# Turning and summing the second half of the positions inside the loop over tiles, ahead of the up-projections

## The chip, the core and the metric

One core of a Trainium2 chip runs the whole program. The metric is the device time of one execution in microseconds (us). Five engines have queues of their own: TensorE (PE in the profile, with its weight loads as PEld), VectorE (DVE), ScalarE (ACT), GpSimd (POOL) and SyncE (SP). SP and POOL issue DMAs here.

## The reference, cut to what matters

Two decoder layers over 1024 positions of 1024 channels. Each ends with a gated feed-forward block, and the change lies at the head of that block, in both layers:

```python
def conv_ffn(h, w_up, dw_w, dw_b, w_down):
    u = causal_dwconv(h @ w_up, dw_w, dw_b)      # (1024 x 1024) @ (1024 x 5632)
    gate, val = jnp.split(u, 2, axis=-1)
    return (jax.nn.silu(gate) * val) @ w_down
...
        h = rmsnorm(x, ffn_norm_g[layer])
        x = x + conv_ffn(h, ffn_w_up[layer], ffn_dw_w[layer], ffn_dw_b[layer], ffn_w_down[layer])
```

## The kernel before

Every matmul operand is kept as two parts, a high one (rounded, written by an ACT cast) and a low one (the rest, usually a DVE subtraction), and a product is three matmuls: high by high, high by low, low by high (`mm3`, L641). A matmul instruction is 128x128 by 128x512.

**The up-projections** (class `Up`) save multiplications with a two-by-two scheme. The activations, turned so that channels lie on the partitions, are four quarters: B11 and B21 are the two halves of the channels for positions 0 to 511, B12 and B22 the same for positions 512 to 1023. Per block `f` of 128 gate and 128 value columns there are seven products of 12 matmuls (four chunks of 128 channels, three matmuls each). Product 0 uses B11, 1 uses B21, 2 uses B22, 3 uses T1 = B11 - B12, 4 uses T2 = B22 + T1, 5 uses T3 = B12 - B22, and 6 uses -T4 = B21 - T2. `hH` and `hL` hold the high and low parts of B11, B21, T1 (in the place of B12) and B22; `self.T` holds those of T2, T3 and -T4. Blocks 0, 1 and 2 start with `first(f)` (product 0, and product 1 in `second`), which need only positions 0 to 511; `block(f)` does the rest.

**Where the quarters come from.** The step before is an output projection with the residual add, in a loop over eight tiles of 128 positions (`back_all`, L780). After each tile's matmuls, DVE adds them to `x` (L808), ACT squares and sums (L716), DVE and POOL make the factor (L709, L710), and DVE scales the tile (L721). Tiles 0 to 3 are then turned by eight 128x128 PE transposes (L258) into two small PSUM banks (`k.sm()`, named ps0bs in the first feed-forward block and ps2s in the second, two banks in turn); ACT and DVE split them and ACT keeps a plain copy in `rb[t]`. Tiles 4 to 7 are left scaled in `ys[t]`. After the loop `turn_rest` turns them into any of eight PSUM banks (`k.bank()`), and DVE writes the four sums into whole-half buffers `raws`, eight instructions of 128x256 per tile. Then T1 and T2 are split by ACT and DVE, and T3 and -T4 by `split_moved`: ACT writes the high part and its negative, and a DMA issued by POOL adds the source onto it.

**The weights** of block `f` are loaded by SP (`load`, L177); `sums` makes the weight sums of the scheme, with ACT (L193, L194) and four accumulating DMAs on POOL (L199).

A scheduler sets the order on each engine ahead of time from its own estimates; on the chip each engine runs its own list strictly in that order, and an instruction that waits holds up all that stand behind it.

Of the kernel before, what the change touches and what calls it, by code (L numbers as in the profile page):

```python
# [23 lines left out]
P = 128  # L24
# [128 lines left out]
class Up:  # L153
# [69 lines left out]
    def norm(self, t, gain):  # L223
# [7 lines left out]
        if t >= 4:  # L231
            self.ys[t] = y[0]
        else:
            self.rb[t] = m.alloc()
            rb, yv = m.ap(self.rb[t]), m.ap(y[0])
            for g in range(2):
# [3 lines left out]
                h = k.hH[:, g * 4:g * 4 + 4, t * P:(t + 1) * P]  # L240
                l = k.hL[:, g * 4:g * 4 + 4, t * P:(t + 1) * P]
# [3 lines left out]
            m.free(y[0])  # L245
        if t in (1, 3):
            self.load(t // 2)
        if t == 6:
            self.prepare(0)

# [9 lines left out]
    def turn_rest(self):  # L260

        k, m, nc = self.k, self.k.m, self.k.nc
        self.prepare(1)
        self.load(2)
        self.prepare(2)
        raws = [[m.alloc() for _ in range(2)] for _ in range(4)]

        def view(i, t):
            return [m.ap(s).rearrange("p (k s) -> p k s", k=2)[:, :, (t - 4) * P:(t - 3) * P] for s in raws[i]]

        def halves(ap):
            v = ap.rearrange("p (k s) -> p k s", k=4)
            return [v[:, 0:2], v[:, 2:4]]

        for t in range(4, 8):
            yv = m.ap(self.ys[t])
            b12, b22 = k.bank(), k.bank()
            self.turn(b12, yv, 0)
            self.turn(b22, yv, 1)
            rb, w = m.ap(self.rb[t - 4]), m.alloc()  # L280
            r22, t1 = m.ap(w)[:, 0:512], m.ap(w)[:, 512:1024]
            nc.scalar.copy(out=r22, in_=b22)
            h = k.hH[:, 4:8, t * P:(t + 1) * P]
            l = k.hL[:, 4:8, t * P:(t + 1) * P]
            v22 = b22.rearrange("p (k s) -> p k s", k=4)
            nc.scalar.copy(out=r(h), in_=v22)
            V = [view(i, t) for i in range(4)]

            def both(eng, out, a, b, op=ALU.subtract):
                for o, x, y in zip(out, a, b):  # L290
                    eng.tensor_tensor(out=o, in0=x, in1=y, op=op)

            both(nc.vector, V[0], halves(rb[:, 0:512]), halves(b12))
            both(nc.vector, V[2], halves(b12), halves(r22))
            both(nc.vector, V[1], halves(b22), V[0], ALU.add)
            both(nc.vector, V[3], halves(rb[:, 512:1024]), V[1])
            nc.vector.tensor_tensor(out=r(l), in0=v22, in1=h, op=ALU.subtract)
            k.banks += [b12, b22]
            m.free(w)
            m.free(self.ys.pop(t))  # L300
            m.free(self.rb[t - 4])
            if t % 2:
                self.first(t // 2 - 2)
        self.first(2)
        self.split_s12(0)
        for i in (0, 1, 2, 3):
            if i == 0:
                for q, s in enumerate(raws[0]):
                    src = m.ap(s).rearrange("p (k s) -> p k s", k=2)
                    h = k.hH[:, q * 2:q * 2 + 2, 512:1024]  # L310
                    l = k.hL[:, q * 2:q * 2 + 2, 512:1024]
                    nc.scalar.copy(out=r(h), in_=src)
                    nc.vector.tensor_tensor(out=r(l), in0=src, in1=h, op=ALU.subtract)
                    m.free(s)
            elif i == 1:
                self.T[i] = [k.split(s) for s in raws[i]]
            else:
                self.T[i] = [self.split_moved(s) for s in raws[i]]
# [48 lines left out]
    def block(self, f):  # L367
# [27 lines left out]
        if f in self.a1:  # L395
            self.second(f)
# [1226 lines left out]
```

## Time and profile before

| | |
|---|---|
| runs, median of 3 | 2321.15 us (2319.4 to 2325.52) |
| profiled execution: time, span | 2319.02 us, 2317.2 us |
| mean granted TensorE clock | 0.993 |
| PE busy | 2232.6 us of the span |
| DVE busy | 1726.5 us |
| ACT busy | 1262.6 us |
| POOL busy | 561.8 us |

The profiled execution stands 2.13 us below the median of the runs. In the first layer the loop over tiles ends at 356.07 us of the span and in the second at 1661.49 us; what follows each, up to the first products that need the second half, is the place of the change. Times in rows of the profile are microseconds from the span's start; a matmul's own duration (0.39) overlaps the next one's, so PE's pace is read from the distance of the starts.

### The profile page before, as it was taken

The numbers are of one execution on the slowest core, as the hardware profiler recorded it, in microseconds if no ns is written. First come the engines' busy times: TensorE is split into PE (matmuls) and PEld (weight loads), VectorE is DVE, ScalarE is ACT, GpSimd is POOL, SyncE is SP. The second block draws the span as 40 slices with busy tenths as digits, with TensorE's granted clock in tenths as the row PEclk, the third lists the DMA queues.
The fourth block names the chain that finished last, engine by engine and source line by source line (L and its number), as shares of the span: only waits on it lengthen the run. The fifth ranks groups of instructions, "written<-read, shape, count | busy, mean of one in ns | idle before, by whom it ended". The sixth has DMA issues, their size and how long they took to land. (4 is left out here: it accounts for less than half of the span.)

```text
span 2317.2 us, 29706 instructions
## 1 busy us (share of the span) xinstructions
PE 2232.6 (96%) x11076; PEld 1908.4 (82%) x11076; DVE 1726.5 (75%) x2023; ACT 1262.6 (54%) x1978; POOL 561.8 (24%) x551
## 2 busy tenths in 40 slices
PE   8998999999999999999999999989999999999999
PEld 8886887888788888889999999978777888888887
DVE  6879457877686887556888888887668777778863
ACT  6433246555555543436677677765566565655341
POOL 2221012111111000035555555562121121110000
PEclk9999999999999999999999999999999999999999
DMA  5984146767676494321111110034476767666812
GB/s 178 190 174 99 35 127 144 191 144 193 148 186 155 146 386 168 103 80 28 37 28 37 37 37 10 28 106 152 130 162 166 192 149 196 145 177 249 332 51 109
DMA packets 247826, 313.00 MB, mean 135 GB/s; under 512 B 12557, under 2 KB 170753, under 8 KB 247681
## 3 DMA queue, kind: packets, MB, share of 16 engines
q1 hardware_dynamic: 214977, 238.32, 31.0%
q0 software_dynamic: 32704, 72.78, 17.7%
q8 instruction: 87, 1.43, 0.2%
q14 instruction: 58, 0.48, 0.1%
HBM read 181.14 MB, written 60.82 MB: 104 GB/s over the span
## 5 line engine op out<-in xcount | busy, mean ns | idle before, releaser
L199 POOL DMA_DIRECT2D t<-t x176 | 155.8, 978 | 701.2 <-ACT t L194 271.3
L628 ACT CAST t<-t 128x1024 fp32r<-128x1024 f32 x178 | 184.9, 1048 | 223.9 <-DMA hs<-t 62.0
L819 DVE SCALAR_TENSOR_TENSOR t<-t,cst,t 128x1023 f32<-128x1023 f32 (+1 forms) x184 | 236.1, 1286 | 81.9 <-ACT t L817 76.7
L629 DVE TENSOR_TENSOR t<-t,t 128x1024 fp32r<-128x1024 f32 x178 | 219.1, 1237 | 101.0 <-ACT t L628 47.2
L1274 DVE TENSOR_TENSOR_SCAN t<-t 128x127 f32<-128x127 f32 (+7 forms) x128 | 204.1, 1600 | 6.9 <-ACT t L1265 6.8
L644 PE MATMUL ps1s<-wH,hH 128*128 128x384 f32 x448 | 165.8, 370 | 0.0
L646 PE MATMUL ps0b<-hH,t 128*128 128x512 f32 x396 | 154.6, 391 | 3.5 <-DVE t L629 3.4
L644 PE MATMUL ps0b<-hH,t 128*128 128x512 f32 x396 | 155.8, 395 | 1.9 <-DVE t L1104 1.4
L645 PE MATMUL ps0b<-hL,t 128*128 128x512 f32 x396 | 154.7, 391 | 0.0
L710 POOL TENSOR_TENSOR stat<-stat,mhalf 128x8 f32<-128x8 f32 (+1 forms) x65 | 80.2, 1234 | 299.9 <-DVE stat L709 299.7
L646 PE MATMUL ps1s<-wH,hL 128*128 128x384 f32 x448 | 151.1, 337 | 0.0
L1279 POOL TENSOR_TENSOR t<-t,t 128x639 f32<-128x639 f32 (+1 forms) x64 | 108.6, 1697 | 175.1 <-DVE t L1274 103.7
L645 PE MATMUL ps1s<-wL,hH 128*128 128x384 f32 x448 | 150.9, 337 | 0.0
L817 ACT ACTIVATE t<-t,cst 128x1024 f32<-128x1024 f32 x88 | 109.1, 1240 | 66.3 <-DVE t L392 47.4
L645 PE MATMUL ps2b<-t,t 128*128 128x512 f32 x342 | 133.9, 392 | 3.9 <-DMA t<-t 3.9
L644 PE MATMUL ps2b<-t,t 128*128 128x512 f32 x342 | 134.0, 392 | 3.3 <-ACT t L394 1.6
L646 PE MATMUL ps2b<-t,t 128*128 128x512 f32 x342 | 132.7, 390 | 0.0
L1265 ACT ACTIVATE t<-ps1s 128x512 f32<-128x512 f32 (+1 forms) x192 | 95.4, 497 | 54.7 <-PE ps1s L1261 28.3
L1297 ACT CAST t<-ps1s 128x512 fp32r<-128x512 f32 (+1 forms) x160 | 87.3, 546 | 60.9 <-PE ps1s L1293 53.5
L1298 DVE TENSOR_TENSOR t<-ps1s,t 128x512 fp32r<-128x512 f32 (+1 forms) x160 | 100.2, 627 | 21.0 <-ACT t L1297 18.8
L517 ACT CAST hH<-t 128x1024 fp32r<-128x1024 f32 x64 | 64.4, 1051 | 86.4 <-PE ps0bs L645 19.6
L517 ACT CAST hL<-t 128x1024 fp32r<-128x1024 f32 x64 | 64.3, 1051 | 86.3 <-PE ps2s L645 25.3
(348 smaller groups left out, 6480.7 us busy)
## 6 DMA issues: line engine op xcount, KB each, us to landing
t<-in_ffn_w_up_dram SPq DMA_DIRECT2D x88, 512.0 KB
t<-t POOLq DMA_DIRECT2D x176, 256.0 KB, 4.4
t<-hs SPq DMA_DIRECT2D x66, 512.0 KB
hs<-t SPq DMA_DIRECT2D x60, 512.0 KB
t<-in_ffn_w_down_dram SPq DMA_DIRECT2D x66, 256.0 KB
xd<-t SPq DMA_DIRECT2D x24, 512.0 KB
wr<-in_attn_w_qkv_dram SPq DMA_DIRECT2D x24, 512.0 KB
t<-in_ffn_w_up_dram SPq DMA_DIRECT2D x44, 256.0 KB
```

Source lines behind the costliest of these rows:

```text
L199: nc.gpsimd.dma_start(out=out, in_=src, accum_op=ALU.add)
L517: nc.scalar.copy(out=r(m.ap(h)), in_=src)
L628: nc.scalar.copy(out=r(m.ap(h)), in_=m.ap(src))
L629: (eng or nc.vector).tensor_tensor(out=r(m.ap(l)), in0=m.ap(src), in1=m.ap(h), op=ALU.subtract)
L644: mm(out=ps, lhsT=sH, rhs=mH, start=start, stop=False, skip_group_check=onto)
L645: mm(out=ps, lhsT=sH, rhs=mL, start=False, stop=False, skip_group_check=onto)
L646: mm(out=ps, lhsT=sL, rhs=mH, start=False, stop=stop, skip_group_check=onto)
L817: nc.scalar.activation(dst, src, AF.Identity, scale=wcols[2], bias=bias)
L819: nc.vector.scalar_tensor_tensor(out=dst[:, s:], in0=src[:, :S - s], scalar=wcols[2 - s], in1=dst[:, s:], op0=ALU.mult, op1=ALU.add)
L1274: self.nc.vector.tensor_tensor_scan(out=rev, data0=rev, data1=rev, initial=1.0, op0=ALU.mult, op1=ALU.bypass)
L1279: self.nc.gpsimd.tensor_tensor(out=B[:, 0:n - 1], in0=B[:, 0:n - 1], in1=K[:, 1:n], op=ALU.mult)
L1298: nc.vector.tensor_tensor(out=r(aL), in0=ps[:, 0:pos], in1=aH, op=ALU.subtract)
```

## The change

Tiles 4 to 7 are turned inside the loop too (`turn_sums`, called from `norm`), into the two small banks. The sums are made in place of what was there: T1 goes over the copy of B11 in `rb`, -T4 over that of B21, T2 and T3 into a new slot, and T1's and B22's parts go to `hH` and `hL` at once. `turn_rest` now issues `first(0)` ahead of the rest and splits T2, T3 and -T4 tile by tile in pieces of 128x256, high by ACT and low by DVE (`split_t`). `split_moved`, with its four accumulating DMAs of 512 KB a layer, is gone, and so is `raws`. Product 1 of block 2 moves from `turn_rest` into `block(0)`.

```diff
@@ norm
-        if t >= 4:
-            self.ys[t] = y[0]
-        else:
+        if t < 4:
...
+        else:
+            self.turn_sums(t, yv, cs)
+        m.free(y[0])
@@
+    def turn_sums(self, t, yv, cs):
+        k, m, nc = self.k, self.k.m, self.k.nc
+        lo, hi = slice(0, 512), slice(512, 1024)
+        b12, b22 = k.sm(), k.sm()
+        self.turn(b12, yv, 0)
+        self.turn(b22, yv, 1)
+        self.ys[t] = m.alloc()
+        rb, w = m.ap(self.rb[t - 4]), m.ap(self.ys[t])
...
+        h1, l1, h2, l2 = k.hH[:, 0:4, cs], k.hL[:, 0:4, cs], k.hH[:, 4:8, cs], k.hL[:, 4:8, cs]
+        tt = nc.vector.tensor_tensor
+        t1 = rb[:, lo]
+        nc.scalar.copy(out=w[:, hi], in_=b22)
+        tt(out=t1, in0=t1, in1=b12, op=ALU.subtract)
+        nc.scalar.copy(out=r(h2), in_=four(b22))
+        nc.scalar.copy(out=r(h1), in_=four(t1))
+        tt(out=w[:, lo], in0=b22, in1=t1, op=ALU.add)
+        tt(out=w[:, hi], in0=b12, in1=w[:, hi], op=ALU.subtract)
+        tt(out=r(l2), in0=four(b22), in1=h2, op=ALU.subtract)
+        tt(out=r(l1), in0=four(t1), in1=h1, op=ALU.subtract)
+        tt(out=rb[:, hi], in0=rb[:, hi], in1=w[:, lo], op=ALU.subtract)
@@ turn_rest
+        self.first(0)
+        self.prepare(1)
+        self.split_t(1, self.ys, slice(0, 512))
+        self.first(1)
+        self.load(2)
+        self.split_s12(0)
+        self.prepare(2)
+        self.split_t(2, self.ys, slice(512, 1024))
+        self.first(2, False)
+        self.split_t(3, [None] * 4 + self.rb, slice(512, 1024))
@@
+    def split_t(self, i, src, half):
...
+        for t in range(4, 8):
+            for j, (h, l) in enumerate(self.T[i]):
...
+                nc.scalar.copy(out=r(h), in_=x)
+                nc.vector.tensor_tensor(out=r(l), in0=x, in1=h, op=ALU.subtract)
@@ block
-        if f in self.a1:
-            self.second(f)
+        for q in (f, f + 2):
+            if q in self.a1 and q in self.done1:
+                self.second(q)
```

The lists show where this puts the instructions. Lines of the changed program differ: L287 is the transpose (L258 before), L795 the residual add (L808), L708 the scaling (L721), L703 the squares (L716), L615 and L616 the high and low part of a whole split (L628, L629), L270 to L278 are in `turn_sums`, L313 and L314 in `split_t`.

PE in the second layer, before, from tile 7's last matmul on. The rows with t23, t37 and t31 turn tiles 4, 5 and 6, each into banks of its own.

```order
L646 MATMUL ps2b2_13163<-t29_12938,t35_13169 128x512
L258 MATMUL ps2b0_13161<-ident_80,t23_13393 128x128 x8
L258 MATMUL ps2b1_13162<-ident_80,t37_13424 128x128 x8
L258 MATMUL ps2s0_13164<-ident_80,t31_13455 128x128 x4
L258 MATMUL ps2s1_13165<-ident_80,t31_13455 128x128 x4
L644 MATMUL ps2b2_13163<-hH_66,t19_13468 128x512
```

PE in the second layer now, 41 rows behind tile 7's last matmul. t19 is tile 6, t35 tile 7; t43 and t35_13623 are the high and low part of a weight of block 1, t49 that of product 3 of block 0.

```order
L631 MATMUL ps2b1_13174<-hH_66,t43_13622 128x512
L632 MATMUL ps2b1_13174<-hL_67,t43_13622 128x512
L287 MATMUL ps2s0_13176<-ident_80,t19_13503 128x128 x4
L287 MATMUL ps2s1_13177<-ident_80,t19_13503 128x128 x4
L287 MATMUL ps2s0_13176<-ident_80,t35_13563 128x128 x4
L287 MATMUL ps2s1_13177<-ident_80,t35_13563 128x128 x4
L631 MATMUL ps2b2_13175<-hH_66,t49_13680 128x512
L633 MATMUL ps2b1_13174<-hH_66,t35_13623 128x512
```

The turns of tiles 4 to 7 still stand behind tile 7's last matmul in this layer, spread among `first` and `second`, and tile 7's go into the banks that tile 6's have just filled.

DVE in the first layer, before, at the scaling of tile 7 (L721).

```order
L291 TENSOR_TENSOR t30_2473<-t38_2149,t37_2469 128x2x128
L291 TENSOR_TENSOR t26_2474<-t38_2149,t45_2470 128x2x128
L721 SCALAR_TENSOR_TENSOR t31_2433<-t23_137,stat_98,t53_2044 128x1024
L629 TENSOR_TENSOR t51_2464<-t39_2450,t42_2463 128x1024
L629 TENSOR_TENSOR t19_2640<-t25_2166,t48_2639 128x1024
```

DVE in the first layer now, at the same scaling (L708). t32_2453 is the low part of block 0's first weight.

```order
L616 TENSOR_TENSOR t32_2453<-t31_2164,t22_2452 128x1024
L277 TENSOR_TENSOR hL_67<-t33_2207,hH_66 128x4x128
L275 TENSOR_TENSOR t21_2435<-ps0bs0_549,t21_2435 128x512
L274 TENSOR_TENSOR t21_2435<-ps0bs1_550,t33_2207 128x512
L276 TENSOR_TENSOR hL_67<-ps0bs1_550,hH_66 128x4x128
L314 TENSOR_TENSOR t46_2657<-t28_2121,t49_2656 128x2x128
L314 TENSOR_TENSOR t46_2657<-t38_2149,t49_2656 128x2x128
L218 TENSOR_TENSOR t16_2771<-t47_2275,t16_2771 128x512
L696 TENSOR_SCALAR stat_98<-stat_98 128x1
```

Tile 7's factor (L696), which stood 8 rows behind tile 7's residual add, now stands 28 rows behind it, and its scaling (L708) six rows further, behind the sums of tiles 5 and 6 and behind splits of T2, T3, -T4 and weights.

ACT in the first layer, before, around tile 7's squares (L716). t39_2450 is the gate weight of block 2, t25_2166 a weight sum of block 0.

```order
L282 COPY t48_2503<-ps0b1_72 128x512
L286 CAST hH_66<-ps0b1_72 128x4x128
L716 ACTIVATE t31_2433,stat_98<-t23_137 128x1024
L193 ACTIVATE t41_2452<-t39_2450 128x512
L194 ACTIVATE t43_2456<-t39_2450 128x1024
L628 CAST t42_2463<-t39_2450 128x1024
L628 CAST t48_2639<-t25_2166 128x1024
```

ACT in the first layer now, ahead of tile 7's squares (L703). t25_2674<-t16_2445 is the high part of another weight sum of block 0, one that POOL's accumulating DMAs have to finish first.

```order
L615 CAST t25_2674<-t16_2445 128x1024
L273 CAST hH_66<-t33_2207 128x4x128
L313 CAST t49_2656<-t28_2121 128x2x128
L313 CAST t49_2656<-t38_2149 128x2x128
L270 COPY t21_2435<-ps0bs1_550 128x512
L272 CAST hH_66<-ps0bs1_550 128x4x128
L217 CAST t16_2771<-t47_2275 128x512
L703 ACTIVATE t31_2487,stat_98<-t23_137 128x1024
```

ACT in the second layer now, ahead of tile 7's squares. t44_13674 is the gate weight of block 2, whose load takes the slot of a weight of the output projection that tile 7 still uses.

```order
L615 CAST t49_13680<-t22_13278 128x1024
L193 ACTIVATE t25_13676<-t44_13674 128x512
L194 ACTIVATE t28_13684<-t44_13674 128x1024
L615 CAST t40_13691<-t44_13674 128x1024
L703 ACTIVATE t35_13563,stat_98<-t43_13070 128x1024
```

In both layers tile 7's squares now stand behind a row of ACT that needs a transfer, and with them, ahead of them or behind, the copies that the turned tiles need.

More of the change, by code (lines that the diff above doesn't have):

```diff
@@ L260, in turn_rest @@
     def turn_rest(self):
-        k, m, nc = self.k, self.k.m, self.k.nc
[L263 to L273, printed above, removed]
-        for t in range(4, 8):
[L276 to L318, printed above, removed]
```

25 lines of the change are left out of this document (13 added, 12 removed).

## The prediction

> **What bounds the kernel now.** First the page's busy times and its chain of waits: TensorE bounds nearly everything.
>
> ```profile
> span 2317.2 us, 29706 instructions
> PE 2232.6 (96%) x11076; PEld 1908.4 (82%) x11076; DVE 1726.5 (75%) x2023; ACT 1262.6 (54%) x1978; POOL 561.8 (24%) x551
> ```
>
> The change adds no matmul and removes none, so it can only move the time that PE loses. I looked for that with PE's waits, between the end of the loop over tiles and the first products that need positions 512 to 1023, in the first layer and then in the second.
>
> ```profile
> PE ps0bs L645 <- DVE hL L313: 2.9, 1, 2.9
> PE ps0bb L644 <- ACT t L394: 2.4, 1, 2.4
> ...
> PE ps2b L645 <- DMA t<-t: 3.9, 1, 3.9
> PE ps2b L644 <- ACT t L394: 1.6, 1, 1.6
> PE ps2b L644 <- DVE t L808: 1.4, 1, 1.4
> ```
>
> The 3.9 is product 6 waiting for the accumulating DMA of -T4, which the change removes. The timeline of PE gives the full loss, slow clock included.
>
> ```profile
> 356.07 1.04 PE L258 MATMUL ps0b<-ident,t 128*128 128x128 f32 x8
> 379.95 0.80 PE L645 MATMUL ps0bs<-hL,t 128*128 128x512 f32 x1 [2.93 <-DVE hL L313]
> 380.97 0.63 PE L644 MATMUL ps0bs<-hH,t 128*128 128x512 f32 x1
> 381.40 0.63 PE L645 MATMUL ps0bs<-hL,t 128*128 128x512 f32 x1
> 400.95 0.50 PE L644 MATMUL ps0bb<-t,t 128*128 128x512 f32 x1 [2.43 <-ACT t L394]
> 401.29 0.39 PE L645 MATMUL ps0bb<-t,t 128*128 128x512 f32 x1
> 403.58 0.39 PE L646 MATMUL ps0bb<-t,t 128*128 128x512 f32 x1
> 403.81 0.39 PE L644 MATMUL ps0b<-hH,t 128*128 128x512 f32 x1
> ...
> 1661.49 1.91 PE L258 MATMUL ps2b<-ident,t 128*128 128x128 f32 x16
> 1666.23 0.50 PE L644 MATMUL ps2b<-hH,t 128*128 128x512 f32 x1 [1.39 <-DVE t L808]
> 1667.35 0.63 PE L644 MATMUL ps2b<-hH,t 128*128 128x512 f32 x1
> 1710.26 0.50 PE L645 MATMUL ps2b<-t,t 128*128 128x512 f32 x1 [3.87 <-DMA t<-t]
> 1711.95 0.63 PE L644 MATMUL ps2b<-hH,t 128*128 128x512 f32 x1
> 1712.37 0.63 PE L645 MATMUL ps2b<-hL,t 128*128 128x512 f32 x1
> ```
>
> At full clock a matmul takes (403.58 - 401.29)/10 = 0.23 us; longer runs give 0.2267, which I use. From 356.07 to the first matmul behind product 6 of block 0 at 403.81 stand 156 matmuls and 32 turns: 156 x 0.2267 + 4 x 1.04 = 39.6 us in 47.74, so 8.1 us are lost. In the second layer the same from 1661.49 to 1711.95 takes 50.5 us, and 10.9 are lost. **No gain of this change at these places can be above 19.0 us.** The rows 0.63 long, 0.42 apart, are slow clock: such stretches are 8 matmuls long and cost 8 x 0.2 = 1.6 us each.
>
> Then a table by stretches, to see who has time where.
>
> ```profile
> core 0: us, PE busy (x) PEld busy (x) DVE busy (x) ACT busy (x) POOL busy (x), PEclk, DMA share, GB/s
> 319.00:356.00 37.00, 37.00 (x180) 30.76 (x179) 19.82 (x25) 17.93 (x30) 6.30 (x9) 1.00 0.49 141
> 356.00:380.00 24.00, 20.98 (x108) 16.89 (x105) 21.24 (x45) 16.07 (x24) 5.93 (x7) 1.00 0.62 135
> 1632.00:1661.00 29.00, 29.00 (x145) 24.34 (x145) 16.16 (x23) 17.30 (x29) 8.22 (x11) 1.00 0.63 165
> 1661.00:1687.00 26.00, 23.59 (x111) 19.03 (x110) 24.89 (x49) 17.76 (x27) 3.88 (x5) 0.93 0.34 81
> ```
>
> In the loop DVE is half busy; behind it DVE is nearly full (21.24 of 24 us, 24.89 of 26). So DVE is the bound at the head, and what matters is whether the change takes DVE work out of it. The durations of that work:
>
> ```profile
> 355.18 1.22 DVE L629 TENSOR_TENSOR t<-t,t 128x1024 fp32r<-128x1024 f32 x1
> 356.31 1.22 DVE L808 TENSOR_TENSOR t<-ps0b,t 128x1024 f32<-128x1024 f32 x1
> ...
> 375.62 1.41 DVE L291 TENSOR_TENSOR t<-ps0b,t 128x256 f32<-128x256 f32 x4
> 381.62 0.68 DVE L363 TENSOR_TENSOR t<-ps0bs,t 128x512 f32<-128x512 f32 x1
> 382.22 0.68 DVE L218 TENSOR_TENSOR t<-t,t 128x512 fp32r<-128x512 f32 x1
> ```
>
> By distance: 1024 wide 1.13 us, 512 wide 0.60, 256 wide about 0.335.
>
> **The change part by part.** Tile by tile, eight sums of 256 columns (2.7 us) and the whole-half splits give way to six instructions of 512 (3.6 us), which hold two splits; `split_t` adds 24 low parts of 256 on DVE (24 x 0.335 = 8.0 us a layer) for T2, T3 and -T4, of which the removed whole splits did T2 and the accumulating DMAs did T3 and -T4. DVE therefore gets more work a layer, at the place where it is the bound, unless the order puts it under the loop. The lists say where it is.
>
> *First layer.* Of tiles 4 to 7 only tile 4 is turned before tile 7's matmuls end; tile 5's turn stands behind them. Tile 7's residual add can start at about 358.3: tile 7's last matmul now ends near 357.5 (8 turn rows of tile 4 are ahead of it), and a low part of a weight, 1024 wide, is in front. From that add up to tile 7's scaling stand 7 DVE instructions of 1024, 14 of 512, 13 of 256 and one tiny: 7 x 1.13 + 14 x 0.60 + 13 x 0.335 + 0.06 = 20.7 us, to 379.0. Then tile 7 is turned, and four of 512 and two of 256 (3.1 us) follow until the small banks are free again, 382.1. Only there can PE go on with the 24 matmuls whose target is such a bank, and then the 84 up to the end of product 6: 108 x 0.2267 = 24.5 us, 406.6. PE's own cover for this, the 48 matmuls and 16 turn rows since 358.2, is 10.9 + 2.1 us, so it waits. To this I add 1.0 us for a stall between products 5 and 6, where the before has one of 2.43 on the same kind of copy (L394); the bounds are 0.6, one copy,
>
> ```profile
> 387.79 0.57 ACT L388 COPY t<-ps0bs 128x512 f32<-128x512 f32 x1
> ```
>
> and 2.43; I take a value nearer the copy, since ACT has less queued there. That makes 407.6 against 403.81: **+3.8 us** (+3.4 to +5.2).
>
> *Second layer.* All four turns stand behind tile 7's last matmul, so nothing of the sums runs in the loop. DVE starts tile 7's add near 1661.9, and up to tile 7's bank-freeing sum it has 7 x 1.13 + 24 x 0.60 + 10 x 0.335 + 0.06 = 25.8 us: 1687.7. PE's cover is 4.2 us of turns and 39 matmuls, 8.8 us, plus what else does not need a small bank; tile 7's turn must wait for tile 6's sums in the same two banks, which I expect as a wait of 4 to 6 us. Behind it stand 117 matmuls, 26.5 us: 1714.2 against 1711.95, **+2.3 us**. The 3.87 at product 6 is gone in this, and DVE is late in its place.
>
> *Transfers in front of ACT.* In both layers tile 7's squares now stand behind an ACT row that needs a transfer. First layer: the cast of t25_2674 needs POOL's four accumulating DMAs of block 0.
>
> ```profile
> DMA to landing us min/median/max: 3.3/4.4/9.6
> ```
>
> They are issued behind an ACT result at about 364.3; with four in a row they land near 370.7, where ACT comes by at 366.9. Late by 0 to 3.5 us; I take 1.5, as the shortest landing would bring them in time. Second layer: the gate weight of block 2 gets its slot at about 1660.3, when tile 7's weight is done. The nearest load in the trace:
>
> ```profile
> 354.43 0.57 SPq L183 DMA_DIRECT2D t<-in_ffn_w_up_dram  x1
> 359.65 0.63 ACT L193 ACTIVATE t<-t 128x512 f32<-128x512 f32 x1 [0.38 <-DMA t<-in_ffn_w_up_dram]
> ```
>
> 5.2 us, so 1665.5 against 1662.4 in line; 0 to 2.6 late behind DVE's queue, I take 1.0. Together **+2.5** (0 to 6.1).
>
> [...]
>
> *Slow clock.* The rows above show it behind waits of 2.93 and 3.87, and not behind 2.43 (401.29 to 403.58 at full pace). Each layer gets a wait longer than that at the turns: 0 to 2 more stretches each, I take one: 2 x 1.6 = **+3.2** (0 to 6.4).
>
> *Parts at nothing.* The removed `split_moved` frees POOL's queue of four DMAs a layer,
>
> ```profile
> L326 POOL DMA_DIRECT2D t<-t x8: 862/872/1170, 383.5 to 1704.7; - x8
> ```
>
> 8 x 0.87 us of a queue that is 24% busy. ACT's 24 casts of 256 stand for whole-half ones and moved copies, and ACT is at 16 to 18 us of 24 to 26 there. The move of product 1 of block 2 changes only which matmuls are cover, and they are counted. The turns are the same 32.
>
> **Sum**: 3.8 + 2.3 + 2.5 + 3.2 = **+11.8 us**. Against the profiled execution's 2319.02 this is 2330.8; that execution stands 2.13 below the median, so the median becomes 2321.15 + 11.8 = 2333.0. The bounds of the terms give +5.7 to +20.0, 2327 to 2341.
>
> **The rivals.** A measurement of this kernel can tell about 0.3%, 7.0 us: no change is 2314.2 to 2328.1.
>
> *No change that can be told.* Transfers land in time and the clock holds: 3.8 + 2.3 = 6.1, 2327.3. Near as likely is that a DVE instruction or two run earlier than my walk has them. For it: both of these terms start at 0, and the trace has ACT waiting only 0.38 on a weight there. Against it: one late transfer is enough to leave the band.
>
> *Faster.* The sums are found done when PE needs them, since the loop's DVE is half idle (19.82 of 37 us): PE never waits, the whole 19.0 goes, 2302; half of it, 2311.6. It decides when the DVE work from tile 7's add to tile 7's sums in the second layer falls from 25.8 us to the 20.5 that 72 matmuls and the turns cover, that is, when nine or more instructions of 512 ran before that add. Against it: the lists put the turns behind tile 7's last matmul, all four in the second layer, three in the first, and an engine runs strictly in its order.
>
> *The change does not do what it says.* In the second layer "in the loop" is after the loop for all four tiles. This is in my forecast; had it been true of the first layer too, that layer would lose tile 4's 3.6 us more: 2336.6.
>
> *More slow clock.* Two more stretches in each layer, since waits for banks come at tile 6's turn and again at tile 7's: 3.2 more than the forecast, 2336.2. For it: 1667.35 is slow behind waits of only 1.39, where turns had stood ahead. Against it: after 356.07 the turns brought none, as the clock of 1.00 in the row from 356 to 380 shows. [...]
>
> **How the numbers follow.** Forecast 0.49, more slow clock 0.09, not in the loop in the first layer either 0.05: slower 0.63. No change 0.24. Faster 0.13. The range runs from 2314, below which the faster case lies, to 2341, the sum of the upper bounds, above which I leave 0.07; the forecast's own range is 2327 to 2341.
>
> **What would show it.** In the second layer, waits of PE at the turns of tiles 6 and 7 on DVE's sums (L275, L276) of 4 to 6 us together; DVE full from 1662 to about 1690; the matmul behind product 6 near 1714 to 1719 instead of 1711.95, and no DMA wait there. In the first layer the same point at 407 to 412 instead of 403.81, with tile 7's scaling near 379 to 381. ACT waits on a DMA just ahead of tile 7's squares. I am wrong if DVE has done tile 5's and 6's sums before tile 7's add, or if later stalls, of blocks 1 and 2, vanish: each gives back what it was long.

## Result: 1.5% slower, and the profile after

| | before | after |
|---|---|---|
| median | 2322.29 us (4 runs, 2319.4 to 2325.52) | 2357.16 us (4 runs, 2355.3 to 2358.4) |
| ratio, 95% interval | | 1.015 (1.0135 to 1.0165) |
| span of the profiled execution | 2317.2 us | 2353.4 us |
| mean granted clock | 0.993 | 0.985 |

The change costs 34.9 us, where the forecast had 11.8 and an upper end of 20. The page of after shows the same matmuls, with PE busy for 10.2 us longer at a lower granted clock, 12 us more of DVE and no more of ACT; the other 26.0 of the 36.2 us by which the span grew are idle time of PE.

```profile
span 2353.4 us, 29690 instructions
PE 2242.8 (95%) x11076; PEld 1913.2 (81%) x11076; DVE 1738.3 (74%) x2039; ACT 1261.6 (54%) x2010; POOL 557.1 (24%) x543
```

**Where it went.** Four rows of each trace cut the program: the first residual add of the loop over tiles, and ACT's last copy of block 0, in each layer. Before, then after:

```profile
310.39 1.23 DVE L808 TENSOR_TENSOR t<-ps0bb,t 128x1024 f32<-128x1024 f32 x1 [5.27 <-PE ps0bb L646]
404.60 0.57 ACT L399 COPY t<-ps0bb 128x512 f32<-128x512 f32 x1
1624.08 2.58 DVE L808 TENSOR_TENSOR t<-ps2b,t 128x1024 f32<-128x1024 f32 x2 [7.07 <-PE ps2b L646]
1712.18 0.59 ACT L399 COPY t<-ps2b 128x512 f32<-128x512 f32 x1 [3.93 <-PE ps2b L646]
```

```profile
310.80 1.23 DVE L795 TENSOR_TENSOR t<-ps0bb,t 128x1024 f32<-128x1024 f32 x1 [5.49 <-PE ps0bb L633]
417.86 0.59 ACT L386 COPY t<-ps0b 128x512 f32<-128x512 f32 x1
1647.49 2.58 DVE L795 TENSOR_TENSOR t<-ps2b,t 128x1024 f32<-128x1024 f32 x2 [7.07 <-PE ps2b L633]
1742.81 0.59 ACT L386 COPY t<-ps2b 128x512 f32<-128x512 f32 x1 [2.13 <-PE ps2b L633]
```

From cut to cut, the after's time less the before's: 12.8 us at the first layer's head, 10.2 behind it, 7.2 at the second layer's head, 5.6 behind it to the end. **The heads lose 20.0 us and the stretches behind block 0, where nothing was forecast, 15.8.** Of the latter, 9.7 and 5.6 us are lost up to the first sum of the down-projection (L571, now L558: 849.17 and 2155.82 before, 872.11 and 2192.06 after), so they lie in the 21 blocks that follow block 0 in each layer. The same four numbers are given for each experiment below. The first add alone stands between 308.7 and 314.8 us in the profiled executions of these kernels, which are the same up to there; so a difference of 2 us in one of them says little, and in the long stretches behind the heads one of 4 us.

**The heads.** PE's waits of after, in the first layer's head and in the second's:

```profile
PE ps0b L633 <- DVE t L616: 8.4, 2, 8.0
PE ps0bs L287 <- DVE t L708: 3.6, 1, 3.6
PE ps0bs L631 <- DVE t L275: 2.2, 1, 2.2
...
PE ps2s L287 <- DVE t L275: 5.2, 1, 5.2
PE ps2b L631 <- ACT t L615: 4.1, 1, 4.1
PE ps2b L631 <- ACT hH L273: 1.7, 1, 1.7
```

Followed back in the timelines of POOL, ACT, DVE and PE of the first layer:

```profile
362.03 1.76 POOL L199 DMA_DIRECT2D t<-t  x2 [3.51 <-PE ps0b L633]
367.66 2.66 POOL L199 DMA_DIRECT2D t<-t  x3 [3.87 <-DMA t<-t]
371.39 0.86 POOL L199 DMA_DIRECT2D t<-t  x1 [1.07 <-DMA t<-t]
...
374.04 1.04 ACT L615 CAST t<-t 128x1024 fp32r<-128x1024 f32 x1 [6.36 <-DMA t<-t]
378.11 1.06 ACT L703 ACTIVATE t<-t 128x1024 f32<-128x1024 f32 x1 [0.41 <-DVE t L616]
...
375.12 1.23 DVE L616 TENSOR_TENSOR t<-t,t 128x1024 fp32r<-128x1024 f32 x1 [4.83 <-ACT t L615]
385.00 1.28 DVE L708 SCALAR_TENSOR_TENSOR t<-t,stat,t 128x1024 f32<-128x1024 f32 x1 [0.46 <-POOL stat L697]
...
378.13 0.80 PE L633 MATMUL ps0b<-hH,t 128*128 128x512 f32 x1 [7.97 <-DVE t L616]
386.35 1.97 PE L287 MATMUL ps0bs<-ident,t 128*128 128x128 f32 x8 [3.58 <-DVE t L708]
417.66 0.39 PE L631 MATMUL ps0bs<-hH,t 128*128 128x512 f32 x1
```

POOL's sums wait for one another. ACT's cast of a sum waits 6.36 us for the third of those issued from 367.66 on; this is the view of that one alone:

```profile
L199 POOL DMA_DIRECT2D t<-t x1: 1433/1433/1433, 368.9 to 368.9; - x1
  ACT t L615: 6.4, 1
DMA to landing us min/median/max: 5.1/5.1/5.1
```

DVE waits 4.83 for that cast, at the head of its line; PE waits 7.97 for the low part of quite another weight that stands behind on DVE. Tile 7's squares (L703) are behind the same cast on ACT, so its scaling comes at 385.00 and its turn at 386.35. The first matmul behind product 6 is at 417.66.

In the second layer ACT waits 2.71 us for the load of block 2, and PE 4.13 behind it. The 5.22 at tile 7's turn ends with DVE, where no row from 1696.14 to 1707.16 had to wait:

```profile
1688.00 0.63 ACT L193 ACTIVATE t<-t 128x512 f32<-128x512 f32 x1 [2.71 <-DMA t<-in_ffn_w_up_dram]
1690.42 1.05 ACT L703 ACTIVATE t<-t 128x1024 f32<-128x1024 f32 x1
...
1690.57 0.53 PE L631 MATMUL ps2b<-hH,t 128*128 128x512 f32 x1 [4.13 <-ACT t L615]
1707.89 1.11 PE L287 MATMUL ps2s<-ident,t 128*128 128x128 f32 x4 [5.22 <-DVE t L275]
1743.07 0.39 PE L631 MATMUL ps2s<-hH,t 128*128 128x512 f32 x1
```

**Behind block 0.** PE's longest wait there, with the rows of ACT ahead of it:

```profile
440.52 0.63 ACT L193 ACTIVATE t<-t 128x512 f32<-128x512 f32 x1 [6.35 <-DMA t<-in_ffn_w_up_dram]
443.67 1.04 ACT L615 CAST t<-t 128x1024 fp32r<-128x1024 f32 x1 [2.51 <-DMA t<-t]
444.62 0.58 ACT L337 COPY t<-ps0b 128x512 f32<-128x512 f32 x1
...
445.25 0.79 PE L631 MATMUL ps0b<-t,t 128*128 128x512 f32 x1 [2.78 <-ACT t L337]
```

ACT has taken up the weight of a block that is wanted only some 50 us later (by the order of the loads block 5; block 4's last copy is at 489.3), waits for its load, and a copy that PE needs now (L337) stands behind it.

### The profile page after: what moved, and what is told of

The parts are those of the page before. It is cut to its first block, busy times and chain, and to the rows that moved or that the text cites. A ratio compares the mean times of both kernels' runs of the same rounds, so it can differ in the third digit from the quotient of the medians.

```text
span 2353.4 us, 29690 instructions
## 1 busy us (share of the span) xinstructions
PE 2242.8 (95%) x11076; PEld 1913.2 (81%) x11076; DVE 1738.3 (74%) x2039; ACT 1261.6 (54%) x2010; POOL 557.1 (24%) x543
## 4 chain that ended last, share of the span: by engine, by line
PE 50%; DVE 15%; DMA 6%; ACT 4%; issue 3%; POOL 3%; SPq 0%; POOLq 0%; DVEq 0%; ACTq 0%
PE ps2b L631 6%; PE ps2b L633 6%; PE ps2b L632 6%; DVE t L1261 4%; PE ps0b L631 3%; PE ps0b L633 3%; PE ps0b L632 3%; PE ps0bb L631 2%; PE ps2s L631 2%; PE ps2s L633 2%; PE ps2s L632 2%; DVE t L806 2%; PE ps0bb L632 2%; PE ps0bb L633 2%; DMA hs<-t 2%
## 5 line engine op out<-in xcount | busy, mean ns | idle before, releaser
L199 POOL DMA_DIRECT2D t<-t x176 | 155.7, 975 | 749.6 <-DMA t<-in_ffn_w_up_dram 303.1
L615 ACT CAST t<-t 128x1024 fp32r<-128x1024 f32 x174 | 181.0, 1048 | 206.3 <-DMA hs<-t 42.6
L616 DVE TENSOR_TENSOR t<-t,t 128x1024 fp32r<-128x1024 f32 x174 | 214.4, 1237 | 81.5 <-ACT t L615 43.2
L804 ACT ACTIVATE t<-t,cst 128x1024 f32<-128x1024 f32 x88 | 109.0, 1240 | 39.6 <-DVE t L349 27.0
L631 PE MATMUL ps2b<-t,t 128*128 128x512 f32 x306 | 119.8, 392 | 2.9 <-ACT t L380 1.4
L632 PE MATMUL ps2b<-t,t 128*128 128x512 f32 x306 | 119.4, 390 | 0.0
L633 PE MATMUL ps2b<-t,t 128*128 128x512 f32 x306 | 118.7, 390 | 0.0
L631 PE MATMUL ps0b<-t,t 128*128 128x512 f32 x272 | 108.6, 399 | 7.2 <-ACT t L380 4.4
L631 PE MATMUL ps2b<-hH,t 128*128 128x512 f32 x260 | 103.4, 398 | 8.0 <-ACT t L615 4.1
```

Of the source, the lines that this page charges most:

```text
L199: nc.gpsimd.dma_start(out=out, in_=src, accum_op=ALU.add)
L615: nc.scalar.copy(out=r(m.ap(h)), in_=m.ap(src))
L616: (eng or nc.vector).tensor_tensor(out=r(m.ap(l)), in0=m.ap(src), in1=m.ap(h), op=ALU.subtract)
L631: mm(out=ps, lhsT=sH, rhs=mH, start=start, stop=False, skip_group_check=onto)
L632: mm(out=ps, lhsT=sH, rhs=mL, start=False, stop=False, skip_group_check=onto)
L633: mm(out=ps, lhsT=sL, rhs=mH, start=False, stop=stop, skip_group_check=onto)
```

## The experiments

Kernels that start from the changed one are named a, those from the kernel before b. Ratios are to the kernel before, run beside them.

| run | median us | ratio (95%) | head 1 | behind 1 | head 2 | behind 2 |
|---|---|---|---|---|---|---|
| after | 2357.16 | 1.015 (1.0135 to 1.0165) | 12.8 | 10.2 | 7.2 | 5.6 |
| a_act_late | 2346.26 | 1.0106 (1.008 to 1.0132) | 6.4 | 3.2 | 5.2 | 9.6 |
| a_second | 2352.31 | 1.0136 (1.0102 to 1.017) | 10.0 | 8.9 | 4.6 | 7.9 |
| a_pool_low | 2355.36 | 1.0146 (1.0116 to 1.0177) | 9.2 | 9.7 | 8.4 | 7.4 |
| a_late_pool | 2348.96 | 1.0111 (1.0091 to 1.0131) | 6.2 | 6.0 | 5.4 | 11.6 |
| a_after_loop | 2341.53 | 1.0078 (1.0059 to 1.0097) | 4.9 | 10.1 | 0.2 | 7.3 |
| a_early2 | 2338.26 | 1.0064 (1.0049 to 1.008) | 0.3 | 11.2 | -1.2 | 8.9 |
| a_late_prep | 2392.65 | 1.0306 (1.0279 to 1.0332) | 6.3 | 30.6 | 5.2 | 28.1 |
| a_late_prep2 | 2340.26 | 1.0076 (1.006 to 1.0093) | 6.3 | 3.2 | 5.2 | 4.7 |
| a_early2_prep2 | 2330.8 | 1.004 (1.0026 to 1.0054) | 1.3 | 2.2 | 1.3 | 4.7 |
| b_second | 2314.74 | 0.9972 (0.9959 to 0.9986) | -1.9 | 4.2 | -0.2 | -2.7 |
| b_split | 2315.95 | 0.997 (0.9959 to 0.9982) | -0.7 | 2.5 | -2.4 | 0.7 |
| b_both | 2315.37 | 0.9971 (0.9956 to 0.9987) | -1.7 | 0.9 | -4.2 | 1.3 |
| b_pieces | 2317.95 | 0.9986 (0.9975 to 0.9996) | 0.8 | 0.3 | -2.1 | -0.2 |
| b_order | 2393.95 | 1.0313 (1.0294 to 1.0331) | 5.5 | 30.9 | 0.8 | 34.5 |
| b_both_prep2 | 2311.67 | 0.996 (0.9946 to 0.9975) | -0.3 | -1.4 | -2.9 | -3.4 |

### Transfers in front of ACT, and DVE's work

**a_act_late** puts the rows that wait for a transfer behind tile 7's last cast on ACT:

```diff
+        with self.k.tc.issue_after(self.last_cast.ins):
+            self.split_s12(0)
+            self.prepare(2)
```

> The changed kernel, with one thing more: on ACT the split of block 0's first weight sum and the preparation of block 2 (negations and split of its weight) are made to stand behind tile 7's last cast, in both layers. Nothing is computed otherwise. Theory 'transfers in front of ACT': the waits of PE of 7.97 us (first layer) and 4.13 us (second layer), which end with ACT results that stood behind a transfer, fall to under 3 and under 1 us, and the time falls by 8 to 14 us from the changed kernel's 2357, to 2343 to 2349. Rival 'DVE is the bound at the head': PE waits the same time elsewhere, at the turns, and the time stays within 4 us of 2357.

Measured: 10.9 us less than the changed kernel. Squares and rows that wait have changed places; PE's wait of 7.97 is 2.54, that of 4.13 is 0.54. The time left the 4 us that the rival allows, but 11.6 us are still lost at the heads, and PE's longest wait in each is at tile 7's turn:

```profile
377.16 1.12 PE L287 MATMUL ps0bs<-ident,t 128*128 128x128 f32 x4 [3.48 <-DVE t L709]
1689.82 1.12 PE L287 MATMUL ps2s<-ident,t 128*128 128x128 f32 x4 [4.62 <-DVE t L275]
```

**a_pool_low** gives DVE less to do:

```diff
+                eng = nc.vector if i == 1 else nc.gpsimd
+                eng.tensor_tensor(out=r(l), in0=x, in1=h, op=ALU.subtract)
-                nc.vector.tensor_tensor(out=r(l), in0=x, in1=h, op=ALU.subtract)
```

> The changed kernel with the low parts of T3 and -T4 made by POOL instead of DVE: 16 subtractions of 128x256 a layer (5.4 us of DVE a layer) leave DVE. Theory 'DVE is the bound at the head': PE's waits at the turns and on splits fall by 3 to 5 us a layer and the time by 6 to 10 us, to 2347 to 2351. Theory 'transfers in front of ACT': only the part of DVE that stands in front of tile 7's turn counts, 0 to 2 us a layer: 2353 to 2357. If POOL is late with its parts, products 5 and 6 wait for POOL and it is slower than 2357.

Measured: 2355.36 (2351.28 to 2360.37), within the second theory's bounds and outside the first's. No wait of PE in the heads ends with POOL.

**a_late_pool** is both edits at once.

> The first experiment's kernel (no transfer in front of tile 7's ACT rows) with the low parts of T3 and -T4 made by POOL, 5.4 us of DVE less a layer. Theory 'DVE is the bound at the head once the transfers are gone': PE's waits at tile 7's turn (3.5 us in the first layer, 4.6 in the second) and on late splits (2.5 and 3.2) fall by 2 to 4 us a layer, the time by 4 to 8 us to 2338 to 2342. Rival 'the two banks and the order of the turns': within 2 us of 2346. If POOL's rows hold up its transfers or tile 7's factor, up to 6 us slower.

Measured: 2.7 us slower than with a_act_late's edit alone, just outside the 2 us of its rival.

But neither run took time off DVE, and so neither tests what less work there would be worth. The 32 instructions that went to POOL should have freed 32 x 0.335 = 10.7 us. DVE is busy for 1737.8 us in a_pool_low against 1738.3 in the changed kernel, and for 1736.6 us in a_late_pool against 1737.4 in a_act_late. Beside POOL's low parts rows of DVE took longer: the two below took 6.19 us together, where two such rows take 0.75 in the changed kernel (from 380.39 on).

```profile
385.37 6.19 DVE L316 TENSOR_TENSOR t<-t,t 128x256 fp32r<-128x256 f32 x2
385.72 5.20 POOL L316 TENSOR_TENSOR t<-t,t 128x256 fp32r<-128x256 f32 x7
```

What DVE's amount of work is worth is read better from b_split, b_pieces and a_early2 below.

### The parts of the change alone, or undone

**a_second** puts product 1 of block 2 back into `turn_rest`, **b_second** makes that move alone.

```diff
-        self.first(2, False)
+        self.first(2)
...
-        for q in (f, f + 2):
-            if q in self.a1 and q in self.done1:
-                self.second(q)
+        if f in self.a1:
+            self.second(f)
```

> The changed kernel with product 1 of block 2 put back from block(0) into turn_rest, the rest as changed. Theory 'late slot': in the changed kernel the gate weight of block 3 goes into a slot that product 1 of block 2 frees (issued at 400.92 us of the span, against 382.93 before), and the first layer's 10 us that are lost behind block 0 come from that. Then block 3's load is issued near 385 us, the loss behind block 0 falls from 10 to under 4 us a layer and the time falls by 6 to 15 us, to 2342 to 2351. Rival 'chance of the lists': the losses behind block 0 come from where the scheduler happens to put rows that wait for weights, in any version; the time changes by less than 5 us, or by as much with stalls at other blocks. Rival 'cover': the 12 matmuls stand again in the head, where they cover 2.7 us of DVE's work a layer: 5 us less, all of it at the head.

> The kernel before with this one part of the change alone: product 1 of block 2 moves from turn_rest into block(0). Theory 'late slot': block 3's gate weight is issued 10 to 18 us later than before, and the kernel is 5 to 15 us slower than before, with waits of ACT on weights and of PE on ACT in blocks 1 to 4. Rival 'chance of the lists': within 5 us of before, and no more wait in blocks 1 to 4 than before has (2.3 us).

Measured: the move alone makes the kernel before 0.3% faster. Undone in the changed kernel it takes 4.9 us off the median; by the table the heads gain 5.4 us and the rest nothing, as the rival 'cover' had it. One of the four runs (2357.87) lies within the changed kernel's, so this gain is little above the noise, and the 5 us of 'chance of the lists' allow it too.

Neither edit moved the load of block 3's gate weight: it goes out at 402.65 with the move undone (400.92 in the changed kernel) and at 382.68 with the move alone (382.93 before). So these two runs do not test 'late slot'. Two others do: a_act_late issues this load at 401.84 and loses 3.2 us behind block 0 of the first layer, a_early2 at 389.52 and loses 11.2. The late load is not what costs.

**b_split** gives T3 and -T4 to ACT and DVE in whole halves:

```diff
-                self.T[i] = [self.split_moved(s) for s in raws[i]]
+                self.T[i] = [k.split(s) for s in raws[i]]
```

> The kernel before with one part of the change alone: T3 and -T4 split by ACT and DVE (whole halves, as T2 is) and no accumulating DMA of POOL for them. DVE gets four instructions of 1024 more a layer (4.5 us), ACT four of 1024 fewer. Theory 'DVE is the bound at the head': the wait of 3.9 us for -T4's DMA in the second layer goes, and 2 to 4.5 us come back at splits in each layer: 2320 to 2326. Rival 'the DMAs cost': 3 to 5 us faster than before, 2316 to 2318. If the change's loss came from this part, it would be 10 us or more slower.

Measured: 2315.95, 0.3% faster, and no wait for -T4's DMA is left. The rival's sign was right: four instructions of DVE more a layer cost less than the accumulating DMAs and the four instructions of ACT that go with them; these two are not separated.

**b_both** joins the two edits, **b_pieces** makes b_both's splits tile by tile:

```diff
-                self.T[i] = [k.split(s) for s in raws[i]]
+                self.T[i] = [(m.alloc(), m.alloc()) for _ in range(2)]
+                for t in range(4, 8):
+                    for q, pair in enumerate(self.T[i]):
...
+                        x = view(i, t)[q]
+                        nc.scalar.copy(out=r(h), in_=x)
+                        nc.vector.tensor_tensor(out=r(l), in0=x, in1=h, op=ALU.subtract)
```

> The kernel before with two parts of the change together: product 1 of block 2 moved into block(0), and T3 and -T4 split by ACT and DVE in whole halves. Each alone was 0.3% faster than before. If they add: 0.5 to 0.7% faster, 2306 to 2312. Theory 'what is left of the loss sits in the in-place sums and the splits by tile': no loss at all behind block 0 here, against 17 us in the kernel with the turns after the loop. Rival 'the moved product and the DVE splits hurt only together': 2325 or more, with waits of PE on ACT in blocks 1 to 4.

> The kernel before with the moved product of block 2, and T2, T3 and -T4 split tile by tile in pieces of 128x256 by ACT and DVE, as in the change, from the whole-half sums of before, behind all turns. Against b_both only the pieces differ: 24 and 24 instructions of 256 in place of 6 and 6 of 1024, by their durations 1.2 us more on DVE and 3 us more on ACT a layer. Theory 'the pieces make the loss behind block 0': 10 us or more slower than b_both, stalls behind copies of ACT in blocks 2 to 4. Rival 'the sums in place and their order': within 4 us of b_both.

Measured: 2315.37 and 2317.95. The two gains do not add; neither loses anything that can be told behind block 0, and the pieces are cleared too. DVE is busy for 7.3 us more than before in b_split and for 10.1 us more in b_pieces, and the heads do not get longer: a fuller DVE need not cost anything there.

**a_after_loop** turns and sums behind the loop, into any bank:

```diff
         # turn_sums
-        b12, b22 = k.sm(), k.sm()
+        b12, b22 = k.bank(), k.bank()
...
         # turn_rest
+        for t in range(4, 8):
+            self.turn_sums(t, m.ap(self.y0[t]), slice(t * P, (t + 1) * P))
         self.first(0)
```

> The changed kernel with tiles 4 to 7 turned and summed after the loop again, into any free bank, as before; the sums in place, the splits tile by tile and the moved product stay as changed. Theory 'two banks': the waits at the turns of tiles 6 and 7 in the second layer (5.2 and 0.7 us) and at tile 7's in the first (2.2) fall below 1 us each, and the time by 4 to 9 us, to 2348 to 2353. Theory 'transfers in front of ACT': tile 7's squares are left where the scheduler puts them; if they stand ahead of the rows that wait for transfers, 8 us less, 2345 to 2350; if behind, no change from 2357. Rival 'in the loop is worth its place': slower than 2357, since tile 4's and tile 5's sums then come out of no loop time, 3.6 to 7 us a layer.

Measured: 2341.53, better than any of the three had it. The wait at a turn did not shrink: PE waits once for 8.6 and once for 8.5 us on a scaling, and still the heads lose only 5.1 us. So the turns lose nothing by leaving the loop, but the waits expected to go did not, and 17.4 us are still lost behind block 0. The edit also writes the turns ahead of `first(0)`; a_early2 below, with the turns in the loop, is 3.3 us faster, and the two intervals overlap. So these runs do not tell whether the loop is the better place.

### The order of writing

`turn_rest` before wrote `prepare(1)`, `load(2)` and `prepare(2)` first; the change wrote them behind `first(0)` and `first(1)`. **a_early2** puts them in front again:

```diff
+        self.prepare(1)
+        self.load(2)
+        self.prepare(2)
         self.first(0)
-        self.prepare(1)
         self.split_t(1, self.ys, slice(0, 512))
         self.first(1)
-        self.load(2)
         self.split_s12(0)
-        self.prepare(2)
```

> The changed kernel with the preparations of blocks 1 and 2 and the load of block 2 in front of the rest in turn_rest, as before the change wrote them. Where they stand decides when the load of block 2 goes out and where ACT prepares it. Theory 'transfers in front of ACT': the wait of ACT for block 2's weight ahead of tile 7's squares in the second layer goes (2.7 us, with PE's 4.1), in the first layer the cast of the weight sum still stands ahead of the squares, so part of the 8 us stays: 3 to 8 us faster than the changed kernel, 2349 to 2354. Rival: no effect, 2357.

Measured: 2338.26, 18.9 us less than the changed kernel, far more than expected: **the loss at both heads is gone** (0.3 and -1.2 us). The turns, the two banks and the sums are the changed kernel's; PE's waits at tile 7's turn in the first layer and at tile 6's in the second are now these, and tile 7's turn in the second waits for nothing:

```profile
377.40 0.77 PE L287 MATMUL ps0bs<-ident,t 128*128 128x128 f32 x5 [0.89 <-DVE t L708]
...
1683.74 0.66 PE L287 MATMUL ps2s<-ident,t 128*128 128x128 f32 x4 [1.20 <-DVE t L275]
1685.53 0.66 PE L287 MATMUL ps2s<-ident,t 128*128 128x128 f32 x4 [1.14 <-DVE hL L276]
1693.57 1.04 PE L287 MATMUL ps2s<-ident,t 128*128 128x128 f32 x8
```

ACT's wait for the weight sum in the first layer is 1.0 us in place of 6.36, and in the second the weight of block 2 is no longer in front of tile 7's squares. But a_act_late had brought that much. There tile 7's scaling in the first layer starts at 375.82 and here at 376.06, no earlier. The difference is on PE: between tile 6's turn and tile 7's stand 32 matmuls here and 10 there, in the second layer 14 and none. So DVE is as busy as in the changed kernel (1737.2 us against 1738.3) and PE has other work while it waits for it. That this cover is what takes the rest of the heads' loss is read from the lists; no run changes it alone.

**b_order** does the reverse to the kernel before: only the order of writing.

```diff
-        self.prepare(1)
-        self.load(2)
-        self.prepare(2)
+        self.first(0)
+        self.prepare(1)
...
-            if t % 2:
-                self.first(t // 2 - 2)
-        self.first(2)
+            if t == 7:
+                self.first(1)
+        self.load(2)
         self.split_s12(0)
+        self.prepare(2)
+        self.first(2)
```

> The kernel before with only the order of writing in turn_rest as the change has it: product 0 and 1 of block 0 first, preparation of block 1 behind them, load and preparation of block 2 behind the turns. Turns, sums and splits as before. In its lists tile 7's squares stay ahead of the rows that wait for transfers. Theory 'the place of the preparations costs by itself': 8 us or more slower than before, at the heads. Theory 'it costs only where tile 7's squares, and with them the turns, fall behind a row that waits': within 6 us of before.

Measured: 72 us slower. The first theory had the sign, but neither had the place or the size: the heads lose 6.3 us; 65.4 are lost behind block 0, 65.0 of them ahead of the first sum of the down-projection in each layer. The same 360 us of the up-projections, of b_order and of before (busy time of PE, PEld, DVE, ACT and POOL with their instructions, then granted clock, share of the DMA engines, GB/s):

```profile
440.00:800.00 360.00, 340.06 (x1457) 271.87 (x1455) 256.44 (x263) 193.03 (x243) 60.23 (x69) 1.00 0.63 157
...
430.00:790.00 360.00, 355.89 (x1561) 291.80 (x1560) 278.53 (x288) 208.75 (x263) 61.29 (x69) 1.00 0.66 167
```

104 matmuls fewer at the same clock, every engine less busy. One of its many waits; 125 us earlier, at 553.27, stands its like:

```profile
677.94 0.58 ACT L389 COPY t<-ps0b 128x512 f32<-128x512 f32 x1 [2.73 <-DVE t L820]
...
678.58 0.50 PE L645 MATMUL ps0b<-hH,t 128*128 128x512 f32 x1 [2.47 <-ACT t L389]
```

Again a copy that PE needs has been held up on ACT, here by waits for DVE. The work is that of the kernel before; the lists are others, and so may be the slots and banks, which are handed out in the order of writing. The run does not separate these two. So an order of writing in the head is enough to set what the 21 blocks behind it do, and to lose there.

### ACT's preparation of later blocks

**a_late_prep** and **a_late_prep2** have a_act_late's edit, and let ACT prepare block f+1 only behind the last copy of block f-1 or f-2:

```diff
-            self.prepare(f + 1)
+            with k.tc.issue_after(self.end_copies[f - 2].ins):
+                self.prepare(f + 1)
```

> The changed kernel with the first experiment's edit (ACT's rows for the weight sum of block 0 and for block 2 behind tile 7's last cast), and one more: in every later block ACT prepares the next block's weight only behind the last copy of the block before, so that no ACT row waits for a weight ahead of a copy that PE needs. Theory 'ACT waits for weights ahead of PE's copies also behind block 0': the 13 us that the first experiment's kernel still loses behind block 0 of the two layers fall to under 5, the time to 2336 to 2341. Rival 'the weights are late by themselves': products then wait for splits instead of copies, and the time stays within 3 us of 2346.

> The first experiment's kernel with ACT's preparation of block f+1 put behind the last copy of block f-2, one block earlier than in the run that lost 46 us. Theory 'ACT's rows wait for weights ahead of copies': the 13 us lost behind block 0 fall to 3 to 8, the time to 2337 to 2342. Rival 'late preparation is what costs': products wait for splits again, 2350 or more.

Measured: the strict rule loses 46 us, which neither had. Products wait for splits, 4.86 us at 438.57 for the first; but here it is the rule that makes ACT late, so the run says nothing of weights that are late by themselves. One block earlier the kernel gains 6.0 us on a_act_late, 4.9 of them behind block 0 by the table, all in the second layer.

**a_early2_prep2** has the preparations in front and the rule of f-2; **b_both_prep2** is the kernel before with its two good parts and that rule.

> The changed kernel with the preparations of blocks 1 and 2 and block 2's load in front again, and ACT's preparation of block f+1 behind the last copy of block f-2. If the preparations' place makes the loss at the heads, and ACT rows that wait for weights ahead of PE's copies make the loss behind block 0 (20 us in the run with the first edit alone), both go: 2322 to 2330, level with before or up to 0.4% slower. Rival 'something else in the in-place sums loses behind block 0': 2334 or more, with PE's waits of 2 to 3.5 us on copies still there at about 433, 472, 1749 and 1787 us.

> The kernel before with the moved product of block 2, the splits of T3 and -T4 by DVE, and ACT's preparation of block f+1 behind the last copy of block f-2. The kernel without the last edit was 0.3% faster than before and lost little behind block 0, so the rule has 2 to 4 us to give: 2309 to 2314. If the preparation comes too late, as with the stricter rule: 2320 or more.

Measured: 2330.8 and 2311.67. In the first the two causes add (18.9 alone by a_early2, 6.0 by the rule): of 34.9 us 26.4 are gone, and the wait at 432.96 of a_early2 has become that at 431.73:

```profile
432.96 0.50 PE L631 MATMUL ps0b<-t,t 128*128 128x512 f32 x1 [3.51 <-ACT t L337]
...
431.73 0.50 PE L633 MATMUL ps0b<-t,t 128*128 128x512 f32 x1 [0.76 <-ACT t L338]
```

It is just above its bound of 2330: some 7 us stay behind block 0, and what holds them was not tried. The second has the lowest median of the study, 0.4% below before (0.25 to 0.54%); its interval overlaps with those of b_split and b_both.

## Why the prediction was wrong

The sign was right; the size was a third of what came. In the profiled executions the heads lose 20.0 us, where the sum had 11.8, and the stretches behind block 0 lose 15.8, where it had nothing.

- **Turns and DVE (+3.8, +2.3).** The picture held for the second layer: the wait at the turns was 5.22 + 0.69 us (4 to 6 forecast), and the point behind product 6 came at 1743.07, which is 1719.7 on the before's clock of that layer (less 23.4, the difference of the first adds; 1714 to 1719 forecast). In the first layer this point came at 417.66, where 407 to 412 was forecast. The walk over DVE's rows was right there too: from tile 7's add at 359.15 to its scaling at 385.00 the rows take 19.9 us, and I had 20.7. I had added up a full DVE as if it never stood still; it stood for 6.0 us, 4.83 of them waiting for ACT, and that is the whole way from 379.0 to 385.0. "DVE is the bound at the head" does not hold as it was meant: b_split and b_pieces give DVE more work and lose nothing, and a_early2 has the changed kernel's DVE work and loses nothing at the heads. (In the sums, 39.6 us at full pace should be 39.5, and DVE's 25.8 us in the second layer 25.7; neither moves the forecast.)
- **Transfers in front of ACT (+2.5, to +6.1): the step that failed first.** I had seen the two rows and priced them at 1.5 and 1.0; ACT waited 6.36 and 2.71, both above the bounds of 3.5 and 2.6. I had let POOL issue four sums in a row, to land near 370.7. Two went out from 362.03 on; the next three could follow only at 367.66, behind the landing of the first; and the one that the cast reads, issued third at 368.9, landed at 374.0. Also the price of such a wait is not its own length: DVE and PE stood behind it with work that had nothing to do with it. Taking both rows away was worth 10.9 us. The first two of these DMAs took 5.2 and 5.8 us from issue to landing, the one that the cast waited for 5.1 and the next 4.1, where the row that I had read before the change has a median of 4.4. Both the line of sums on POOL and the time of the one that mattered were longer than I had them.
- **The order of writing: not in the sum at all.** My list of parts at nothing went through the moved product, the removed DMAs, ACT's casts and the turns. That `prepare(1)`, `load(2)` and `prepare(2)` had moved behind `first(0)` stood in the diff, and I priced only what the lists showed of it in the head. By a_early2 it is 18.9 of the 34.9 us, all of the heads' loss. This is not a loss beside that of the transfers: a_act_late, which leaves the writing and only reorders ACT, takes 8.4 us of the same 20.0 away. The rest goes with the matmuls that the order puts ahead of the turns, as far as the lists tell.
- **Nothing behind product 6: the sum ended too early.** 15.8 us were lost behind block 0, 15.3 of them in the 21 blocks of each layer. The lists are others there, and I did not walk them. Shown: rows of ACT that wait, ahead of copies that PE needs (a_late_prep2, a_early2_prep2 against a_early2), and that the order of writing alone can do this (b_order). Open: why the scheduler makes such lists of the one order and not of the other, and the last 7 us.
- **Slow clock (+3.2).** Gaps of 0.38 to 0.50 us between matmuls number 14 and 16 at the two heads, 8 and 9 before: 13 x 0.2 = 2.6 us, and 0.9 more for the eight turns that took 1.97 us and not 1.04. The size was right. One reading was not: the turns behind 356.07 in the first layer before were taken to show that turns keep the clock up. They stand in lots of at most ten (1.24 us, from 360.35 on) with matmuls between, and the wait of 2.43 us, without any work, brought no slow clock there either; so they show nothing of that either way.
- **Parts at nothing.** In the kernel before, the removed DMAs and the moved product are each a gain of 0.3% by themselves, and the splits in pieces do no harm. In the changed kernel the moved product rather costs, by a_second, probably since its matmuls are missed as cover in the head.

Of the rivals none came about; the slowest of them, at 2336.6 us, was still 20.6 us short. With the preparations in front, the turns in the loop cost nothing at the heads, but they gain nothing either.

## What to carry to other kernels

Where a scheduler lays out the lists, the order of writing is part of a change: compare the lists to their end, not only where the edit is. On every engine look for rows that wait for a transfer and ask what stands behind them; the price is that of the most urgent row behind, not of the wait (here 10.9 us for two rows that waited 6.36 and 2.71). And before an engine is called the bound because it is full, see what the waiting engine could do in the meantime. Taking work off the full engine is a test only if its busy time falls; here work moved from DVE to POOL came back as longer rows of DVE.

## What the runs showed of the hardware

The slow clock of TensorE lasted longer than the 8 matmuls that I had read from the trace before. Behind the wait of 7.97 us the ten matmuls from 378.13 on and the seven from 390.54 on stand 0.43 us apart behind a first gap of 0.59, with eight turns between them that take 1.97 us and not 1.04. The granted clock was 0.50 in all three stretches (378.20 to 382.20, 386.30 to 388.40, 390.60 to 393.60) and 1.00 from 394.00 to 398.00, where matmuls are 0.23 us apart again, behind these rows:

```profile
382.13 0.63 PE L633 MATMUL ps0b<-hH,t 128*128 128x512 f32 x1
...
393.27 0.63 PE L631 MATMUL ps0bs<-hH,t 128*128 128x512 f32 x1
393.69 0.47 PE L632 MATMUL ps0bs<-hL,t 128*128 128x512 f32 x1
394.00 0.39 PE L633 MATMUL ps0bs<-hH,t 128*128 128x512 f32 x1
```

The 4.0 us of matmuls without a pause from 378.13 to 382.13 did not bring full pace back; it came 3.2 us into the next stretch, and a wait of 3.6 us, the turns and a wait of 2.2 us lay between.

Accumulating DMAs of POOL (L199, 256 KB each) took 3.2 us from issue to landing at least, 4.3 in the median and 10.0 at most in the changed kernel.

Where subtractions of 128x256 ran on POOL (a_pool_low, a_late_pool), DVE was busy for only 0.5 and 0.8 us less, though rows of 10.7 us had been taken off it; the rows of DVE that ran beside POOL's took 11.8 and 9.6 us longer in sum than the medians of their kind.
